# Two middle loads of x merged into one of six rows per partition, in a batch norm and ReLU kernel

## The chip, the cores and the metric

The kernel runs on one core of one Trainium2 chip. The metric is the device time of one execution in microseconds (us). All timed runs quoted here are in the fast state; runs taken once beside a profile have no state and are marked so. Kernels are compared only within the same rounds.

A ratio below is the mean time of one kernel's fast runs over the mean of the kernel before's fast runs of the same rounds, with a 95% interval. So it is not quite the ratio of the medians that stand beside it.

## The reference

```python
# x: (32, 128, 32, 32) float32; gamma, beta, running_mean, running_var: (128,)
normalized = (x - running_mean[None, :, None, None]) / np.sqrt(running_var[None, :, None, None] + eps)
scaled = normalized * gamma[None, :, None, None] + beta[None, :, None, None]
return np.maximum(scaled, 0).astype(np.float32)
```

16.78 MB are read and as many written. The arithmetic is one ReLU with a scale and a bias per channel.

## The kernel before

x is seen as two halves `t`. In each half a partition holds 16 rows of 1024 floats (4 KB), contiguous in DRAM. A row is one channel of one image, so each row has its own scale and bias. `PIECES` says which rows go in one load; `STORE_CUTS` adds places where a store ends inside a piece.

```python
J = 16
PIECES = (((0, 2), (2, 4), (4, 8), (8, 16)), ((0, 8), (8, 16)))
STORE_CUTS = {(0, 1)}
...
    for t in range(T):
        for a, b in PIECES[t]:
            xt = data.tile([P, b - a, HW], F32, name=f"x{t}_{a}")
            nc.sync.dma_start(out=xt, in_=xr[t, :, a:b, :])          # loads: queue of SP
            tiles.append((t, a, b, xt))
    raw = params.tile([Q, 4, J], F32, name="raw")
    for k, src in enumerate((running_var, gamma, running_mean, beta)):
        nc.scalar.dma_start(out=raw[:, k, :], in_=src.rearrange("(q j) -> q j", j=J))   # queue of ACT
    ...   # matmul spreads the parameters to 128 partitions; sqrt, reciprocal: scale_t, bias_t
    with tc.manual_schedule(engines={mybir.EngineType.Activation}):
        for t, a, b, xt in tiles:
            first = a
            for j in range(a, b):
                nc.scalar.activation(out=xt[:, j - a, :], in_=xt[:, j - a, :], func=ACTF.Relu,
                                     bias=bias_t[:, j : j + 1], scale=scale_t[:, j : j + 1])
                if j + 1 == b or (t, j + 1) in STORE_CUTS:
                    nc.scalar.dma_start(out=outr[t, :, first : j + 1, :],
                                        in_=xt[:, first - a : j + 1 - a, :])   # queue of ACT
                    first = j + 1
```

## Time and profile before

| | before |
|---|---|
| time | 83.73 us, median of 3 (83.72 to 83.98) |
| span in the profile | 81.9 us |
| ACT busy | 38.5 us (47%) |
| DMA engines: loads / the other queue | 48.4% / 47.8% of the span |
| first ReLU starts / last store issued | 9.72 / 55.97 us |

Two things help in reading the DMA lines. A packet of this trace is one partition's row of one DMA, so 128 packets make a load of x, eight on each of the 16 DMA engines. And in a stretch of the DMA view a packet counts, with its whole time, where it starts. A stretch in which sixteen packets of one kind start, about one per engine, gives their mean time as share times length. Here are the last data packets of the last load, 44.5 to 45.0 us (columns: packets, MB, share of 16 engines):

```profile
q1 hardware_dynamic: 16, 0.52, 242.6%
```

2.426 x 0.5 = 1.213 us for each 32 KB packet. This is also the median over all 32 KB packets of the trace, loads and stores.

### The profile page before, as it was taken

What the parts mean: (1) busy time and instruction counts of PE and PEld (TensorE: products, weight loads), DVE (VectorE), ACT (ScalarE), POOL (GpSimd) and SP (SyncE); (2) the same over time, 40 slices, a digit from 0 to 9 for tenths busy, and PEclk for the clock granted to TensorE, in tenths of its full rate; (3) what the DMA queues carried; (4) which work ended last, traced back from release to release, by engine and by line L of the source; (5) the groups of instructions that cost most, each with busy time, mean ns of one, the idle gap of its engine ahead of it and who ended that gap; (6) DMA issues with size and microseconds to landing.
All of it is one profiled execution on the core that took longest, in us unless ns stands there. A gap on an engine that the chain in (4) does not pass through costs nothing.

```text
span 81.9 us, 119 instructions
## 1 busy us (share of the span) xinstructions
PE 0.7 (1%) x2; PEld 0.5 (1%) x2; DVE 0.8 (1%) x5; ACT 38.5 (47%) x34; POOL 0.8 (1%) x6
## 2 busy tenths in 40 slices
PE   0002000000000000000000000000000000000000
PEld 0002000000000000000000000000000000000000
DVE  0000300000000000000000000000000000000000
ACT  0600377799039999199994199993000000000000
POOL 3000000000000000000000000000000000000000
DMA  2899999989899999979789798996999899799690
GB/s 32 328 425 472 408 448 448 512 352 494 370 448 416 446 418 396 500 296 600 320 380 580 304 464 384 512 512 288 480 512 400 368 512 448 320 512 496 272 512 0
DMA packets 1936, 33.56 MB, mean 410 GB/s; under 512 B 272, under 2 KB 272, under 8 KB 528
## 3 DMA queue, kind: packets, MB, share of 16 engines
q1 hardware_dynamic: 864, 16.78, 48.4%
q10 hardware_dynamic: 1072, 16.78, 47.8%
HBM read 16.78 MB, written 16.78 MB: 410 GB/s over the span
## 4 chain that ended last, share of the span: by engine, by line
DMA 56%; ACT 11%; SPq 0%; issue 0%
DMA x<-in_x_dram 56%; ACT x L96 11%; SPq L52 0%
## 5 line engine op out<-in xcount | busy, mean ns | idle before, releaser
L96 ACT ACTIVATE x<-x,bias_t,scale_t 128x1024 f32<-128x1024 f32 x32 | 37.0, 1228 | 10.3 <-DMA x<-in_x_dram 7.9
L82 ACT ACT_TABLE_LOAD x1 | 1.3, 1283 | 2.6 <-issue 2.6
L82 ACT ACTIVATE std_t<-cols,eps_t 128x16 f32<-128x16 f32 x1 | 0.3, 273 | 4.5 <-PE cols L74 4.5
L74 PE MATMUL cols<-raw,rep 8*128 8x64 f32 x2 | 0.7, 428 | 7.7 <-DMA raw<-in_beta_dram 7.7
L74 PEld LDWEIGHTS cols<-raw,rep 8*128 8x128 f32 x2 | 0.5, 304 | 7.7 <-issue 7.7
L64 POOL TENSOR_SCALAR_AFFINE_SELECT rep<-rep 8x128 f32<-8x128 f32 x1 | 0.4, 392 | 0.1
L84 DVE RECIPROCAL rstd_t<-std_t 128x16 f32<-128x16 f32 x1 | 0.3, 254 | 7.8 <-ACT std_t L82 7.8
L63 POOL MEMSET rep<- 8x128 f32 x1 | 0.2, 195 | 0.3 <-POOLq L124 0.3
L86 DVE TENSOR_TENSOR scale_t<-cols,rstd_t 128x16 f32<-128x16 f32 x1 | 0.2, 175 | 0.1
L90 DVE TENSOR_TENSOR bias_t<-cols,ms_t 128x16 f32<-128x16 f32 x1 | 0.2, 175 | 0.0
L88 DVE TENSOR_TENSOR ms_t<-cols,scale_t 128x16 f32<-128x16 f32 x1 | 0.2, 175 | 0.0
L124 POOL MEMSET const-bfloat16-1.0<- 128x1 bf16 x1 | 0.1, 106 | 0.0
L124 POOL MEMSET const-uint8-127<- 128x1 uint8 x1 | 0.1, 106 | 0.0
L124 POOL MEMSET const-float32-0.0<- 128x1 f32 x1 | 0.1, 103 | 0.3 <-issue 0.3
L124 POOL MEMSET const-float32-1.0<- 128x1 f32 x1 | 0.1, 103 | 0.0
L61 DVE MEMSET eps_t<- 128x1 f32 x1 | 0.1, 59 | 0.9 <-PEq L124 0.9
## 6 DMA issues: line engine op xcount, KB each, us to landing
x<-in_x_dram SPq DMA_DIRECT2D x3, 4096.0 KB, 38.8
out_dram<-x ACTq DMA_DIRECT2D x3, 4096.0 KB, 27.9
x<-in_x_dram SPq DMA_DIRECT2D x2, 1024.0 KB, 5.7
x<-in_x_dram SPq DMA_DIRECT2D x1, 2048.0 KB, 11.2
out_dram<-x ACTq DMA_DIRECT2D x1, 2048.0 KB
out_dram<-x ACTq DMA_DIRECT2D x2, 512.0 KB, 18.8
out_dram<-x ACTq DMA_DIRECT2D x1, 1024.0 KB
raw<-in_running_var_dram ACTq DMA_DIRECT2D x1, 0.5 KB
```

The source lines that it names most:

```text
L61: nc.vector.memset(eps_t, float(eps))
L63: nc.gpsimd.memset(rep, 1.0)
L64: nc.gpsimd.affine_select(out=rep, in_=rep, compare_op=mybir.AluOpType.is_equal, fill=0.0, base=0, pattern=[[0, P // Q], [-1, Q]], channel ...
L74: nc.tensor.matmul(cols.rearrange("p k j -> p (k j)"), rep.rearrange("q r s -> q (r s)"), raw.rearrange("q k j -> q (k j)"), start=True, s ...
L82: nc.scalar.activation(out=std_t, in_=cols[:, 0, :], func=ACTF.Sqrt, bias=eps_t[:, 0:1], scale=1.0)
L84: nc.vector.reciprocal(out=rstd_t, in_=std_t)
L86: nc.vector.tensor_mul(out=scale_t, in0=cols[:, 1, :], in1=rstd_t)
L88: nc.vector.tensor_mul(out=ms_t, in0=cols[:, 2, :], in1=scale_t)
L90: nc.vector.tensor_sub(out=bias_t, in0=cols[:, 3, :], in1=ms_t)
L96: nc.scalar.activation(out=xt[:, j - a, :], in_=xt[:, j - a, :], func=ACTF.Relu, bias=bias_t[:, j : j + 1], scale=scale_t[:, j : j + 1],)
L124: nc = _bacc.Bacc("TRN2", target_bir_lowering=False, num_devices=1)
```

## The change

One load fewer, with the store pieces kept by a new cut: rows 2-4 and 4-8 of the first half come as rows 2-8.

```diff
-PIECES = (((0, 2), (2, 4), (4, 8), (8, 16)), ((0, 8), (8, 16)))
+PIECES = (((0, 2), (2, 8), (8, 16)), ((0, 8), (8, 16)))
-STORE_CUTS = {(0, 1)}
+STORE_CUTS = {(0, 1), (0, 4)}
```

## The prediction

> **What bounds the kernel now.** I read the page first: busy shares, the forty slices, the DMA queues. In sections 2 and 3 of the page of the kernel before:
>
> ```profile
> span 81.9 us, 119 instructions
> ...
> DMA  2899999989899999979789798996999899799690
> ...
> DMA packets 1936, 33.56 MB, mean 410 GB/s; under 512 B 272, under 2 KB 272, under 8 KB 528
> ## 3 DMA queue, kind: packets, MB, share of 16 engines
> q1 hardware_dynamic: 864, 16.78, 48.4%
> q10 hardware_dynamic: 1072, 16.78, 47.8%
> ```
>
> The shares of the two queues (q1 loads x, q10 carries the parameters and the stores) add to 96.2% of the 16 DMA engines over the whole span: 0.962 x 81.9 = 78.8 us of transfer in an 81.9 us span. The busiest compute engine, ACT, has 38.5 us. So the DMA engines are the bound. The 3.1 us left lie at the two edges: in the first two slices (2 and 8 tenths) and the last one.
>
> The chain of work that ended last, read second, seems to say otherwise:
>
> ```profile
> by line: DMA x<-in_x_dram 55.6%; ACT x L96 11.2%; SPq L52 0.5%; issue 0.2%
> ...
> 1.23 6.74 DMA x<-in_x_dram
> ...
> 7.99 38.77 DMA x<-in_x_dram
> ...
> 46.79 9.16 ACT x L96 x8
> ```
>
> It goes through the second load of x (the one to be merged), but only because the sixth load was issued when the second had landed at 7.97. That link is not a cause of time. At 7.99 the load queue still held the third, fourth and fifth load, and the sixth needed 38.77 us because it stood behind them. The chain also stops at 55.95, at the last ReLU, and names nothing for the 26 us after it. So I asked the DMA view for what ran from the end of the loads to the end of transfer:
>
> ```profile
> DMA packets 559, 14.42 MB, mean 427 GB/s; under 512 B 63, under 2 KB 63, under 8 KB 63
> ...
> q10 hardware_dynamic: 559, 14.42, 98.9%
> ```
>
> This is 46.8 to 80.6: 14.42 of the 16.78 MB of stores run here, with the engines 98.9% full. The last store was issued at 55.97 (its row below). Its 4.19 MB take 9.8 us at 427 GB/s, so its turn came near 80.6 - 9.8 = 70.8. It waited some 15 us behind earlier stores. That is the slack of ACT at the end. Hence the model: end = first packet + bytes over the rate + tail, as long as one of the two queues always has work.
>
> **The start, where the change acts.** The timeline, third:
>
> ```profile
> 2.08 0.45 ACTq L59 DMA_DIRECT2D raw<-in_beta_dram  x1
> ...
> 7.73 0.65 PE L74 MATMUL cols<-raw,rep 8*128 8x64 f32 x2 [7.73 <-DMA raw<-in_beta_dram]
> ...
> 9.72 1.24 ACT L96 ACTIVATE x<-x,bias_t,scale_t 128x1024 f32<-128x1024 f32 x1 [1.03 <-DVE bias_t L90]
> ...
> 55.97 0.34 ACTq L104 DMA_DIRECT2D out_dram<-x  x1
> ```
>
> The first ReLU does not wait for x but for the parameters: beta, 512 bytes, was issued at 2.08 and let the matmul go only at 7.73. The DMA view of 4.9 to 7.5 shows why:
>
> ```profile
> DMA packets 200, 1.16 MB, mean 448 GB/s; under 512 B 67, under 2 KB 67, under 8 KB 67
> ## 3 DMA queue, kind: packets, MB, share of 16 engines
> q1 hardware_dynamic: 152, 1.16, 106.0%
> q10 hardware_dynamic: 48, 0.00, 1.2%
> ```
>
> Each parameter load uses eight partitions: 8 data packets and 8 completion packets. The first one's 16 went before 2.0. The other three's 48 go in exactly this stretch, which is the stretch of the second load of x. On an engine that is 6 small packets, each with one 8 KB packet of x ahead of it.
>
> **What the Trainium skill says.** "DMA: Bandwidth & Descriptors", section "Queues, rings and completion order": an engine takes turns between the queues that have work, packet by packet. The trace agrees in kind: three parameter loads need six turns. In this trace a packet is one partition's row, 8 to 32 KB, so a turn gets longer with the row. The same page, section "Where 436 GB/s comes from", gives a ceiling of 435.2 GB/s for the 16 ports; the trace has 427 in the store stage, so next to nothing is to be had in rate. Its section "Measured" has 341 GB/s for 1 MB and 425 for 16 MB (another issuing path), with the rule to batch. That speaks for merging, but it is for a load timed alone. Here the second 1 MB load runs in a full queue, and its stretch moved 448 GB/s (a little high, since a packet counts where it starts). No loss there for a merge to win back.
>
> **The change part by part.** Loads of rows 2-4 and 4-8 (packets of 8 and 16 KB) become one of rows 2-8 (24 KB). The listing of instructions of both kernels shows the same 32 ReLUs and the same seven stores in the same order; the new entry among the store cuts keeps the pieces.
>
> 1. Packets. From the DMA view of 3 to 4 us: 52 packets of 8 KB at a share of 100.7%, so 16 x 1.007 / 52 = 0.310 us each. From 8 to 12: 108 packets of 16 KB at 103.1%, so 64 x 1.031 / 108 = 0.611 us. Per 8 KB that is 0.301 and a fixed 9 ns; a 24 KB packet should take 0.912 us (estimate). Per engine, removed 8 x (0.310 + 0.611) = 7.37 us, added 8 x 0.912 = 7.30 us: -0.07 us. One completion packet of some 10 ns goes too. Sum on the bound: -0.08 us.
> 2. Issue. SP issues one DMA fewer, some 0.4 us of its own time, while the queue is full: 0.
> 3. Semaphores. Loads 4, 5 and 6 had to wait for the variance, the mean and the second load of x; now loads 4 and 5 wait for gamma and beta. Beta will come late (step 4), near 11.4 us, when at most 4.2 MB of the 12.6 MB issued have moved. The queue stays full: 0.
> 4. Parameters. Each of the six turns now stands behind a 24 KB packet: 6 x (0.912 - 0.310) = 3.6 us. The matmul moves from 7.73 to about 11.3 and the first ReLU from 9.72 to about 13.3. This is the largest thing the change does. On the path that sets the end it costs nothing: loads fill the engines meanwhile.
> 5. The wait for x. Bytes ahead of row 2's arrival grow from 2 to 4 MiB, so it lands when the old third load did: issued near 1.7, plus the 11.2 us to landing that the page gives for the 2 MB load, 12.9 instead of 7.97. The ReLUs reach it at 13.3 + 2 x 1.7 = 16.7 (1.7 from one ReLU's start to the next, 9.72 to 11.42, with the store's issue between): no wait.
> 6. Later. ReLUs of rows 2-8 end near 16.7 + 2.37 + 0.42 + 4.63 = 24.1 (20.53 before; two ReLUs, an issue gap, four ReLUs as in the timeline of before), so those of rows 8-16 begin near 24.6 instead of 23.86, and their wait of 3.32 us for the load all but vanishes. About three store turns fewer pass before the loads are done, so the last load lands earlier, by 0.5 to 1.5 us, and the last store is issued near 55. The bytes not stored then are stored later: sum 0.
>
> Total: 83.73 - 0.08 = 83.65 us. The spread of the three runs before (83.72 to 83.98) is larger than this gain; I say 83.7.
>
> **The rivals.**
> A. The delayed parameters reach the end: all of 3.6 us is paid, 87.3. For it: ACT is on the chain of waits and starts late. Against: 15 us of slack at the last store, and ACT idles 7.9 us in three waits for x, which swallow the shift by the third.
> B. The merge frees the chain's link at 7.97 and the sixth load comes earlier, for a gain of one to two us (82). Against: the 38.77 us are queueing, the engines are full from the third slice on; no bytes leave.
> C. Rows of 24 KB run slower than 8, 16 or 32 KB. At a quarter slower 8 packets x 0.23 = +1.8 us (85.5). No such packet is in this trace; the three sizes that are lie on one line, so I give it little.
> D. A start with fewer and larger pieces leaves the store queue empty later on, +0.5 or more. Against: after 46.8 it holds 14.4 MB.
>
> **Range and chances.** My theory gives 83.65, and run spread is about 0.2. A and C in part could put it up to 84.2, a luckier start down to 83.35. So 83.7, range 83.35 to 84.15. Two per cent is 1.67 us: faster needs bytes or gaps removed that are not there (0.01), slower needs C or A nearly whole (0.02), within 0.97.
>
> **What would show it right or wrong.** Step 1: q1 with 144 packets fewer (720), shares adding to 96% again. Step 4: first ReLU at 12.8 to 14; if it stays at 9.7, the turn-taking is misread. Step 6: the wait before rows 8-16 under 0.5 us, the last ReLU ending before 56, and stores still filling the engines to about 80.5. A is right if the last store starts to move as soon as it is issued; C if the 24 KB packets take clearly over 0.91 us; a stretch of slices under 8 in the middle would break the whole model.

## The result and the profile after

| | before | after |
|---|---|---|
| time, median of 6 | 83.77 us (83.72 to 84.06) | 84.34 us (84.26 to 84.6) |
| ratio | | 1.0064 [1.0044, 1.0084] |
| span in the profile | 81.9 us | 82.5 us |

The kernel became 0.6% slower. That is within 2%, but outside the predicted range of 83.35 to 84.15, and clear of the spread. From the page of the changed kernel:

```profile
span 82.5 us, 118 instructions
...
DMA  2898997999797989898979999998996998999690
...
DMA packets 1792, 33.56 MB, mean 407 GB/s; under 512 B 256, under 2 KB 256, under 8 KB 512
...
q1 hardware_dynamic: 720, 16.78, 48.7%
q10 hardware_dynamic: 1072, 16.78, 47.4%
```

The packets went down by 144, as they should, and no slice in the middle has gone idle. The two queues together still fill 96.1% of the span. But multiply the shares by the spans: the load packets took 0.484 x 81.9 = 39.6 us per engine before and 0.487 x 82.5 = 40.2 now; the other queue 39.1 both times. So the 0.5 us or so are in the packets of the loads: the same bytes took longer.

The start of the changed kernel, in the timeline:

```profile
11.23 0.66 PE L74 MATMUL cols<-raw,rep 8*128 8x64 f32 x2 [11.23 <-DMA raw<-in_beta_dram]
...
13.22 1.24 ACT L96 ACTIVATE x<-x,bias_t,scale_t 128x1024 f32<-128x1024 f32 x1 [1.02 <-DVE bias_t L90]
...
24.45 9.16 ACT L96 ACTIVATE x<-x,bias_t,scale_t 128x1024 f32<-128x1024 f32 x8 [0.42 <-ACT x L96]
...
55.52 0.34 ACTq L104 DMA_DIRECT2D out_dram<-x  x1
```

The parameters come 3.5 us later, as forecast, and so does the first ReLU. The wait of 3.32 us before rows 8-16 is gone, and the last store is issued earlier than before. The DMA view of 9 to 10 us gives the new row size:

```profile
q1 hardware_dynamic: 16, 0.39, 91.7%
q10 hardware_dynamic: 8, 0.00, 0.6%
```

0.917 us per 24 KB packet (0.912 was estimated). Eight of the small parameter packets still pass between them. Now the last data packets of the last load, 43.4 to 44.0 us:

```profile
q1 hardware_dynamic: 16, 0.52, 282.3%
q10 hardware_dynamic: 13, 0.11, 41.8%
```

2.823 x 0.6 = 1.69 us each, against 1.213 before. All sixteen are stretched, 1.61 to 1.85 us. That alone is 0.48 us per engine, most of the loss.

### The profile page after: what moved, and what is told of

It reads as the page before. It is cut to its first block, busy times and chain, and to the rows that moved or that the text cites. A ratio compares the mean times of both kernels' runs of the same rounds, so it can differ in the third digit from the quotient of the medians.

```text
span 82.5 us, 118 instructions
## 1 busy us (share of the span) xinstructions
PE 0.7 (1%) x2; PEld 0.5 (1%) x2; DVE 0.8 (1%) x5; ACT 38.5 (47%) x34; POOL 0.8 (1%) x6
## 3 DMA queue, kind: packets, MB, share of 16 engines
q1 hardware_dynamic: 720, 16.78, 48.7%
q10 hardware_dynamic: 1072, 16.78, 47.4%
HBM read 16.78 MB, written 16.78 MB: 407 GB/s over the span
## 4 chain that ended last, share of the span: by engine, by line
DMA 54%; ACT 11%; ACTq 1%; issue 0%
DMA x<-in_x_dram 43%; ACT x L96 11%; DMA raw<-in_beta_dram 11%; ACTq L59 1%
## 6 DMA issues: line engine op xcount, KB each, us to landing
x<-in_x_dram SPq DMA_DIRECT2D x1, 3072.0 KB, 11.7
```

## The experiments

### Which theories

Two theories at first. *Late start*: the merged load as such is harmless, but the late parameters start ReLUs and stores 3.5 us later, and something in the later meeting of stores and loads stretches load packets. *The merge itself*: 24 KB rows or the missing load cost. A third was chance.

The table sums up all runs. "Stretch" is worked out from the packet records of each trace: the time of a 32 KB load packet beyond 1.213 us, averaged over the 16 engines and summed over the 8 packets of the load of rows 8-16 ("first", where the stores begin), the next 14 ("middle") and the last 2 ("last"). One profile each.

| run | first ReLU, us | stretch first / middle / last, us | median, us | ratio |
|---|---|---|---|---|
| before | 9.7 | 0.13 / 0.06 / 0.00 | 83.77 | 1 |
| before, second profile (e18) | 9.7 | 0.29 / 0.20 / 0.02 | 83.95, one run | |
| changed | 13.2 | 0.21 / 0.04 / 0.56 | 84.34 | 1.0064 |
| changed, again (e1) | 13.0 | 0.30 / 0.12 / 0.56 | 84.34 | 1.0040 |
| before, ReLUs late (e5) | 10.5 | 0.29 / 0.12 / 0.30 | 84.21 | 1.0028 |
| before, ReLUs late (e6) | 11.7 | 0.37 / 0.02 / 0.61 | 84.47 | 1.0059 |
| before, ReLUs late (e2) | 13.1 | 0.37 / 0.07 / 0.56 | 84.51 | 1.0066 |
| before, ReLUs late (e4) | 16.7 | 0.33 / 0.13 / 0.57 | 84.46 | 1.0057 |
| the same as e2, halves swapped (e11) | 12.7 | 0.35 / 0.17 / 0.34 | 84.45 | 1.0065 |
| merged, 8 KB rows (e12) | 9.7 | 0.24 / 0.05 / 0.02 | 83.84 | 0.9991 |
| merged, parameters on the load queue (e3) | 9.7 | 0.34 / 0.01 / 0.02 | 84.86 | 1.0119 |
| before, one more store cut (e14) | 9.6 | 0.35 / 0.00 / 0.68 | 84.54 | 1.0068 |
| e2 with larger first stores (e13) | 13.2 | 0.81 / 0.07 / 0.00 | 84.10 | 1.0020 |
| merged, no cuts (e16) | 12.9 | 0.80 / 0.17 / 0.00 | 84.52 | 1.0072 |
| merged, old cut only (e17) | 12.9 | 0.31 / 0.93 / 0.00 | 85.09 | 1.0142 |
| one queue, before (e7) | 9.3 | 0.02 / 0.11 / 1.33 | 84.95 | 1.0120 |
| one queue, merged (e8) | 12.8 | 0.02 / 0.02 / 1.48 | 84.74 | 1.0097 |
| one queue, halves swapped (e9) | | 0.01 / 0.00 / 1.35 | 84.77, one run | |
| one queue, big rows first (e15) | 22.5 | 0.00 / 0.28 / 1.37 | 84.97, one run | |
| one queue, stored backwards (e10) | | 0.00 / 0.00 / 0.00 | 94.36, one run | |

All were correct.

### Is it chance? The changed kernel and the kernel before again (e1, e18)

No edit in either.

> The changed kernel once more, unedited. In its first profile the 0.6 us over the prediction sits in load packets of 32 KB that took longer than 1213 ns while stores ran beside them, most of all in sixteen packets that started between 43.4 and 43.9 us and took 1.61 to 1.85 us. If the stretch belongs to the schedule: 84.3 us again (ratio 1.006) and the same sixteen packets stretched at 43.4 to 43.9. If it is chance (a refresh, a disturbance): the stretch is elsewhere or absent in this profile, and the time wanders.

The changed kernel again took 84.34 us (84.2 to 84.43; ratio 1.004 [1.0015, 1.0065]). In the DMA view of 43.7 to 44.0 us of that run:

```profile
q1 hardware_dynamic: 16, 0.52, 556.9%
```

5.569 x 0.3 = 1.67 us: the same sixteen packets, at the same time, on another execution. It belongs to the schedule.

> The kernel before once more, unedited, for a second profile: how much of the stretch repeats. Expected: none on the last packets of the last load (0 in the first profile), 0.1 to 0.4 us around the first store packets (0.13 in the first), span 81.8 to 82.1.

Span 82.1 us, one run at 83.95. The last packets were again unstretched (0.02 us for the last two), and the stretch around the first stores was 0.29 instead of 0.13, with 0.20 instead of 0.06 in the middle. So two profiles of one kernel differ by some 0.3 us in these two places together, and small differences there mean nothing. The third number repeated to 0.02 in both kernels that were profiled twice.

### Late ReLUs without the merge (e2, e4, e5, e6)

```diff
+    idle = params.tile([P, 1024], F32, name="idle")
+    nc.vector.memset(idle, 0.0)
     with tc.manual_schedule(engines={mybir.EngineType.Activation}):
+        for n in (1024, 1024, 1024):      # e2; one in e5, two in e6, six in e4
+            nc.scalar.activation(out=idle[:, :n], in_=idle[:, :n], func=ACTF.Relu, bias=bias_t[:, 0:1])
```

> The kernel before, its loads untouched, with three idle ReLUs of 128x1024 that read the bias ahead of the first real one, so that the first real ReLU starts near 13.2 us as in the changed kernel. Theory 1 (the late start of ReLUs and stores costs, by where stores meet loads): near 84.3, ratio 1.005 to 1.007, stretched load packets. Theory 2 (the merged load itself costs): 83.8, ratio 1.000 +- 0.002.

> The kernel before with six idle ReLUs, first real ReLU near 16.6 us. Theory 1a (cost grows with the delay, since fewer stores overlap loads): 84.8 to 85.0, ratio 1.012. Theory 1b (only the alignment of store turns and load packets counts): anything from 83.6 to 84.4, not in proportion. Theory 2: 83.8. In all, the last store still starts to move long after its issue, so none expects 3.5 us or more.

> The kernel before with one idle ReLU, first real ReLU near 10.9 us. When the last packets of the last load run, about 21 store packets per engine have gone (22 in the kernel before, 18.6 in the changed one). If the loss is a step between there: 83.8 to 84.0 and no stretch of the last load packets. If it grows with the delay: ratio 1.002.

> The kernel before with two idle ReLUs, first real ReLU near 12.0 us, about 20 store packets per engine at the last load packets. If the loss is a step it lies on one side or the other: 83.8 or 84.4. If it grows with the delay: ratio 1.004.

With its loads untouched and only its first ReLU moved to 13.1, the kernel before took 84.51 us, ratio 1.0066 [1.0045, 1.0088]: the whole loss of the change. First the timeline of e2, then its DMA view of 43.7 to 44.3:

```profile
13.11 1.23 ACT L100 ACTIVATE x<-x,bias_t,scale_t 128x1024 f32<-128x1024 f32 x1
```

```profile
q1 hardware_dynamic: 16, 0.52, 254.7%
q10 hardware_dynamic: 11, 0.09, 35.4%
```

2.547 x 0.6 = 1.53 us, on the same last packets of a load that nobody edited. The four delays give a curve. A delay of 0.8 us costs 1.0028 [1.0012, 1.0044], of 2.0 us 1.0059 [1.0037, 1.0081], of 3.4 us 1.0066, and of 7.0 us 1.0057 [1.0027, 1.0087]. The cost is full after 2 us and then stays. So it isn't the delay, paid in part; a later start brings it on. A clean step was not found either: 0.8 us gave about half. That fits the last column of the table (0.30 against 0.56 to 0.61).

### The merge without the delay (e3, then e12)

e3 put three parameter loads on the load queue, between the first and the second load of x, and two idle ReLUs to bring the first real one back to 9.7:

```diff
-            nc.scalar.dma_start(...)    # gamma, mean, beta on the queue of ACT
+            if (t, a) == (0, 0):
+                for k in range(1, 4):
+                    nc.sync.dma_start(out=raw[:, k, :], in_=small[k].rearrange("(q j) -> q j", j=J))
```

> The changed kernel with gamma, mean and beta issued from the load queue between the first and the second load of x, so that they do not stand behind 24 KB packets, and idle ReLUs of 1024 and 512 columns that put the first real ReLU back near 9.7 us. Theory 1: 83.7, ratio 0.998 to 1.001, little stretch. Theory 2: still 84.3, ratio 1.006.

84.86 us, ratio 1.0119 [1.0085, 1.0154]: neither theory. Its last load packets are not stretched (0.02), as *late start* has it, but the edit brought a cost of its own. In the DMA view of 80.6 to 82.4 us:

```profile
DMA packets 16, 0.03 MB, mean 18 GB/s; under 512 B 15, under 2 KB 15, under 8 KB 15
```

Beside fifteen completion packets, one store packet of 32 KB starts in there. It ends at 82.29, the one before it at 81.53: no other engine took it over, and the one that is behind sets the end. The packet records show the engines falling out of step where the small loads pass, at 4.6 us (24 KB packets of 0.91 to 1.87 us start there). The profiled execution was a long one, 85.41 us of 84.68 to 85.45, so this lag may be smaller in the others. As a test of the merge this run is spoiled.

e12 keeps the merged load and the parameters where they are. It pads the tile in SBUF, so that the load's rows go as three packets of 8 KB per partition instead of one of 24. The store of rows 4-8 then goes as two packets of 8 KB per partition instead of one of 16 (its edit is left out here):

```diff
-            xt = data.tile([P, b - a, HW], F32, name=f"x{t}_{a}")
-            nc.sync.dma_start(out=xt, in_=xr[t, :, a:b, :])
+            # for rows 2-8 only
+            xt = data.tile([P, 3, 2 * HW + 16], F32, name=f"x{t}_{a}")
+            nc.sync.dma_start(out=xt[:, :, : 2 * HW],
+                              in_=xr[t, :, a:b, :].rearrange("p (g r) w -> p g (r w)", r=2))
```

> The changed kernel, with the merged load's tile padded so that its 24 KB per partition go as three packets of 8 KB (and the store of rows 4-8 as two of 8 KB). One load fewer, as in the change, but the parameter packets stand behind 8 KB again. Theory (the late start is what costs, not the merge): first ReLU at 9.7, 22 or more store packets per engine done at the last load packets, no stretch there, 83.8 us, ratio 0.998 to 1.002. Rival (the merge costs by itself): 84.3.

83.84 us, ratio 0.9991 [0.9974, 1.0007]. The timeline, and the DMA view of 44.4 to 44.9:

```profile
9.68 1.24 ACT L106 ACTIVATE x<-x,bias_t,scale_t 128x1024 f32<-128x1024 f32 x1 [1.02 <-DVE bias_t L97]
```

```profile
q1 hardware_dynamic: 16, 0.52, 246.6%
q10 hardware_dynamic: 6, 0.05, 23.2%
```

1.233 us. One load fewer, nothing late, nothing lost. The changed store is no way out of this reading: up to the last load packets the same stores have gone as in the kernel before (16 packets of 4 KB and 6 of 8 KB per engine). With e2 this settles the first question: in this form the merge costs nothing and gains nothing that the runs could show; the 24 KB rows in front of the parameter packets make the ReLUs late, and the late start is what costs.

### Addresses, or the place in the order? (e9, e11)

```diff
-            nc.sync.dma_start(out=xt, in_=xr[t, :, a:b, :])
+            nc.sync.dma_start(out=xt, in_=xr[1 - t, :, a:b, :])     # and outr[1 - t, ...] in the stores
```

> The late-ReLU form of the kernel before (three idle ReLUs) with the two halves exchanged in DRAM. Place in the order: last packets stretched by 0.5 us or more together, 84.4 us, ratio 1.005 to 1.008. Addresses: no stretch there, 83.8 us.

> The one-queue form of the kernel before with the two halves of x and out exchanged in DRAM (loads and stores alike), so that the last two packets of each engine's last load read other addresses. If the stretch of those packets (0.95 and 0.38 us on average in the one-queue run) belongs to the place in the order: again 0.8 us or more on the last two, 84.9 us. If it belongs to the addresses: the last two at 1213 ns, and the stretch is in the second-last or the fourth load, or gone.

With the halves of x exchanged in DRAM the last packets stretch all the same: e11 took 84.45 us, ratio 1.0065 [1.0047, 1.0082], with 0.34 us on the last two (less than the 0.5 expected). e9 is the swapped form of e7, described next; its last two gave 1.35 us against 1.33. So the place in the order counts, not these addresses.

### No turns at all: loads and stores on one queue (e7, e8, e10, e15)

```diff
-                    nc.scalar.dma_start(out=outr...
+                    nc.sync.dma_start(out=outr...        # stores stand behind the loads
# e10 besides: for t, a, b, xt in reversed(tiles)
# e15 besides: for t, a, b, xt in tiles[3:4] + tiles[:3] + tiles[4:]
```

> The kernel before with its seven stores issued on the load queue, behind the loads, so that no store packet takes turns with a load packet. Theory (the loss is load packets stretched while stores run beside them): no 32 KB load packet over 1250 ns, 83.55 us, ratio 0.996 to 0.999, since the kernel before has only 0.2 us of such stretch. Rival (it comes from elsewhere, such as the issue of stores or the ReLUs' traffic): 83.8 or more.

> The changed kernel with its stores behind the loads on one queue. The parameters are still late and the first ReLU still near 13.2. Theory: all of the 0.6 us comes back, 83.5 us, ratio 0.995 to 0.999, the same as the kernel before in that form or 0.08 us less. Rival (the merged load itself costs): 0.5 us above that kernel.

> The one-queue form with the ReLUs and stores in reverse order of the loads, so that nothing can be stored, nor stands in the queue, until the last load has landed and eight ReLUs have run: some 92 us, on purpose. If the last load's packets stretch because store packets stand right behind them: all at 1213 ns here. If the end of the load order alone stretches them: again 0.8 us or more.

> The one-queue form with the rows of 32 KB processed and stored first, so that the packets right behind the last load are of 32 KB. Small packets: the last load's packets at 1213 to 1300 ns and 83.6 to 83.9 us (1.3 us less stretch than the one-queue run). Any store behind the loads: stretched by 0.8 us or more again.

The expectation for e7 and e8 was wrong. They were to be the cure and took 84.95 us (1.012 [1.0105, 1.0135]) and 84.74 us (1.0097 [1.0082, 1.0112]). The stretch is no matter of loads and stores taking turns: with no store packet before 42.4 us, the last two packets of the last load stretched more than in any run with two queues. The DMA view of e7, 38.5 to 41.4, and then of e10, 38.5 to 41.0:

```profile
q1 hardware_dynamic: 32, 1.05, 129.4%
```

```profile
q1 hardware_dynamic: 32, 1.05, 97.0%
```

In e7 32 packets give 1.294 x 2.9 / 2 = 1.88 us each; in e10, 0.970 x 2.5 / 2 = 1.21. The two differ in what stands behind the loads on the queue. In e10 nothing does, since no store can be issued before eight ReLUs of the last tile have run, and none of its 384 load packets of 32 KB is stretched by more than 0.002 us in the mean of any sixteen. (Its 94.36 us are the price of an idle DMA for 10 us, on purpose.) In e10 no ReLU runs beside the loads either, but that is not it: in e7 ReLUs ran beside the earlier loads from 9.3 us on, and these packets hardly stretched (0.02 and 0.11). So store work that stands ready behind the last loads stretches them. e15 asked whether small packets must stand there: with 32 KB packets next it still stretched, 1.37 us. In one queue 4 or 32 KB made no difference.

### With two queues: which stores stand next? (e14, e13, e16, e17)

In the kernel before 22 store packets per engine have gone when the last load packet starts, and of the 4 and 8 KB stores only two are left (8 + 8 + 8 in all). After a late start (e2, e4, the changed kernel) 16 to 19 have gone and five or more are left.

e14 leaves more small packets with nothing late, by one more cut:

```diff
-STORE_CUTS = {(0, 1)}
+STORE_CUTS = {(0, 1), (0, 3)}
```

> The kernel before with one more store cut, rows 2 and 3 stored apart: nothing is late (first ReLU 9.7), 22 to 23 store turns at the last load packets, but there some nine packets of 4 KB still wait to go before the 16 KB ones. Small packets waiting: stretch of 0.5 us or more on the last load packets and ratio 1.005 to 1.009, without any delay. Number of turns or lateness: 83.8, ratio 1.000.

84.54 us, ratio 1.0068 [1.0049, 1.0087]. In the DMA view of 43.7 to 44.3:

```profile
q1 hardware_dynamic: 16, 0.52, 265.8%
q10 hardware_dynamic: 13, 0.05, 21.5%
```

1.59 us. First ReLU at 9.6, 21.8 store packets per engine gone, and yet the full loss. So lateness is only one way to get there: 4 KB stores up to the end of the loads are another. That doesn't mean that any small stores left over are enough: e12 speaks against it. There 18 store packets of 8 KB per engine were left at the last load packets, more small ones than in any run of this section or of the delays, and the stretch of the last two load packets was 0.02 us. The DMA view of e12 at 46.2 to 51.1, after the loads:

```profile
q10 hardware_dynamic: 272, 2.10, 101.1%
```

These are 256 packets of 8 KB, 16 per engine, and 16 completion packets.

e13 is the reverse, late but with larger stores next: `STORE_CUTS = set()` in e2, so that its stores have rows of 8, 8, 16 and 32 KB.

> The late-ReLU form of the kernel before (first real ReLU near 13 us) without the store cut, so that the two 4 KB stores become one of 8 KB rows. About 19 store packets per engine are again gone at the last load packets, but those that stand next are of 16 KB (five left, then 32 KB) instead of 8 KB. If the stretch needs small store packets waiting behind the last loads: no stretch there, ratio 0.998 to 1.002. If it only needs few store turns to have passed: stretch of 0.6 us again, ratio 1.006.

84.10 us, ratio 1.002 [1.0001, 1.0039]. The DMA views of e13 at 46.2 to 47.3 and at 18 to 19:

```profile
q1 hardware_dynamic: 16, 0.52, 110.6%
```

```profile
q1 hardware_dynamic: 16, 0.52, 150.8%
```

The last packets are at 1.217 us, so that part is gone. But a stretch has come up where the stores begin: 1.51 us. Two thirds of the loss in time are won back, not all.

e16 and e17 tried to use this on the changed kernel: no cuts (stores of 8, 24, 32 KB), and only the old cut (4, 4, 24, 32 KB).

> The changed kernel without store cuts: stores of 8, 24 and 32 KB rows. The start is as late as in the change. Store turns are longer, so the last load lands near 55 instead of 46 and the last store is issued near 65, still before its turn (70.8). Small packets: no stretch, 83.5 to 83.8 us, ratio 0.996 to 1.000, perhaps the fastest. Lateness alone: 84.3.

> The changed kernel without the store cut that the change added: stores of 4, 4, 24 and 32 KB rows. The start is as late as in the change, and the stores begin with 4 KB packets as there; at the last load packets some 18 store turns have gone and 24 KB packets stand next. If the loss has two places, at the first store packets and, when small packets remain, at the last load packets: the second is gone (under 50 ns), the first stays, 83.8 to 84.1 us, ratio 1.000 to 1.003. If lateness alone sets it: 84.4, ratio 1.006.

Both missed: 84.52 us (1.0072 [1.0051, 1.0093]) and 85.09 us (1.0142 [1.012, 1.0163]). The DMA view of e16 at 52.2 to 53.3, then of e17 at 38.8 to 40.0:

```profile
q1 hardware_dynamic: 16, 0.52, 110.3%
```

```profile
q1 hardware_dynamic: 16, 0.52, 142.4%
```

In both the end of the loads is clean (1.213 us in e16; 0.00 for the last two in e17). In e16 the stretch sits at the first stores (0.80), in e17 in the middle: 1.424 x 1.2 = 1.71 us, just where the 4 KB stores end and the 24 KB ones begin. So avoiding the stretch at the end of the loads moved it to an earlier place. No version of ours beats the kernel before; e12 equals it.

### What the runs have in common, and what stays open

Every large stretch lies where the stores' part in an engine's traffic steps up: from none to the first packets, from 4 KB to 24 KB rows, or, at the end of the loads, from one packet of 4 or 8 KB per 32 KB load packet to nothing but stores. From none to 4 KB it is 0.13 to 0.37 us, from none to 8 KB 0.8, from 4 to 24 KB 0.9, from none to all 1.3 to 1.5 (the one-queue runs). In the kernel before the sum of all three is 0.2 to 0.5. But not every step stretches, and its size doesn't rank the runs: at the end of the loads turns of 4 KB gave 0.57 (e4) and 0.68 (e14), and turns of 8 KB anything from 0.00 (before) and 0.02 (e12) to 0.61 (e6). One count does separate the runs with two queues: the KB of stores that an engine had done by the last load packets. It is 110 or more in the runs with 0.02 us or less there, 104 in e5 (0.30) and 64 to 94 in the rest (0.34 to 0.68). It was found afterwards, and no run tests it. All this describes the runs and was made after most of them; e17 was not foreseen. What happens inside the DMA engine there is open: no view shows more of a packet than its queue, start, time and size, and we don't know why a load packet, and not the store packet, carries the time. Nor does the stretch account for the time to the tenth: e13 has 0.88 us of it and lost 0.17 us, e16 has 0.98 and lost 0.6.

## Why the prediction was wrong

Its range missed the time by 0.2 us, and the direction was missed too: a gain of 0.08 us was forecast and 0.57 us were lost. By its steps:

1. Packets: right. 720 load packets; a 24 KB packet 0.917 us. Summed from the packet records, the 8, 16 and 24 KB load packets took 10.20 us per engine against 10.28, the 0.08 us of the forecast. The 32 KB ones, which nobody edited, took 29.93 against 29.30.
2. Issue and 3. semaphores: right. No gap in the load queue followed.
4. Parameters: right in size (3.6 us forecast, 3.5 measured: matmul at 11.23, first ReLU at 13.22). **The step that failed is its last sentence: "On the path that sets the end it costs nothing: loads fill the engines meanwhile."** The engines were full, but a full engine did less. e2, which has this delay and nothing else, has the whole loss (1.0066).
5. The wait for x: right. No wait before the third ReLU.
6. Later: the 3.32 us wait vanished and the last store was issued at 55.52, as said. "The bytes not stored then are stored later: sum 0" is the same error. When the stores stand at another point as the loads run out, the last load packets take 1.69 instead of 1.21 us. The last load was to land 0.5 to 1.5 us earlier; its ReLUs began 0.45 us earlier (46.34 against 46.79).

Behind both stands the model, "end = first packet + bytes over the rate + tail, as long as one of the two queues always has work". It takes a packet's time to depend on its size alone. The trace of the kernel before invited this: its last load packets were at 1.213 us. But that kernel's store pieces happen to fit its start time.

The rivals: A was rightly put aside; the last store was issued 0.45 us earlier than before, not later. B and C fell as argued. D, an empty store queue, is not what happened either: from 46.0 to 81.3 the stores fill 99.2% of the engines:

```profile
q10 hardware_dynamic: 642, 15.09, 99.2%
```

C alone named slower packets in a full engine, and put them in the 24 KB rows; none of the four named the unchanged 32 KB packets. The sign to look for, "shares adding to 96% again", could not have shown it, since stretched packets count as busy. The test that does is busy time per byte: 39.6 against 40.2 us for the same 16.78 MB.

## What to carry to other kernels

When the DMA engines are full, ask not only whether the queue ever runs empty but how long each packet takes: multiply a queue's share by the span and compare kernels on the same bytes. A row size that is made larger in one queue delays every small transfer that takes turns with it (six parameter packets: 3.5 us here), and a schedule whose stores happen to fit the end of its loads can lose 0.6% by that delay alone. If loads are merged to save issues, keep the packets small (padding the tile did it: 0.9991), and don't expect a gain while the queue is full.

## What the Trainium skill lacked or had wrong

- "DMA: Bandwidth & Descriptors", section "Queues, rings and completion order": turns by packet are right, but here a packet was one partition's row of 4 to 32 KB (128 packets per load of x), so the length of a turn goes with the row. Six turns took 3.5 us longer behind 24 KB rows than behind 8 KB rows.
- The same page, sections "Rules for kernel authors" and "Measured", asks for at least 1 MiB per DMA, which both loads had before the change; its table goes on from 341 GB/s at 1 MB to 425 at 16 MB. It lacks that this is no promise inside a full queue: there the merge of a 1 MB and a 2 MB load gained nothing (0.9991 [0.9974, 1.0007]), and with longer packets it lost 0.6%.
- The same page, section "Issuing engines are not separate DMA queues", says that issuing from several engines only saves sequencer time. With all stores behind all loads on one queue, instead of on two that take turns, the same work took 84.95 against 83.96 us (1.012), and the loss was in the transfers: 1.33 us of stretch on the last two load packets.
- No page has it that load packets can stretch when stores stand ready behind them: a 32 KB load packet took 1.213 us elsewhere and 1.4 to 2.3 us there (e7), on all 16 engines at once.
- No page says what became of e3: three loads of 512 bytes placed between large loads on the same queue left one engine 0.76 us behind the next at the end of the profiled execution (85.41 us; median 84.86, 1.0119).
